# Two accumulator banks begun in spare PSUM banks, the old four copied out together, and one more unit by sums in the last round of the down projection

## The chip, the cores and the metric

One core of a Trainium2 chip runs the whole program. The metric is the device time in microseconds (us). TensorE (PE) does the matrix products; VectorE (DVE) and ScalarE (ACT) prepare its operands and move its results; GpSimd (POOL) issues the accumulating DMAs; SyncE (SP) issues the weight loads. The program gives each engine its instructions in a fixed order, so one that waits holds up those behind it on that engine.

## The reference

A block of one layer on 256 tokens of width 2048, all in float32:

- h = x + GLA(rmsnorm(x)), a chunked gated linear attention with its projections
- a = relu(rmsnorm(h) @ w_up), with w_up of 2048 x 8192
- h = h + (a * a) @ w_down, with w_down of 8192 x 2048
- the output is rmsnorm(h)

The change lies wholly in the product with w_down.

## The kernel before

**Operands in two parts.** Every weight tile is loaded as float32 into a tile `raw`. ACT casts it to `hi` (L118), DVE subtracts to get `lo` (L131 for plain loads, L165 for w_up, L998 for sums), and PE makes three products, hi*hi, lo*hi and hi*lo (L719). `raw` has seven buffers, used in turn; `hi` and `lo` have five.

**The order of the two projections.** The hidden width is cut into 8 rounds of 1024. `up()` makes the activations of a round in 16 steps; `down()` multiplies them with w_down. A round of `down` takes four groups g of 512 output columns, one pass per group, and each pass takes four units kp of 256 hidden rows. In the last round only g = 0 and g = 1 are done in this way; the other 1024 columns follow in eight steps of 128 rows, `last_step` (L1084), whose matmuls have line L176. `up` runs 18 steps ahead; while it has steps left, one up step is laid between the products of each unit, and at the end the units stand alone. In the code `alone` (L911) is true for these.

**A unit in two ways.** A plain unit makes eight block products, 24 matmuls of 256 columns. A unit *by sums* (`by_sums`, L694) makes seven, 21 matmuls, on four accumulators P16, B32, P57 and BX4 of one PSUM bank each (L858). It needs sums of weight blocks: a second DMA on POOL's queue adds one block onto another while loading (L934), DVE makes three more additions (L957 to L959), ACT casts the sums (two casts of 512 columns, L991), and DVE subtracts once more over 1024 columns (L998). The first nine matmuls use the plain blocks (`these`, L951), the other twelve the sums (`early` and `late`, L999 and L1000). For a unit that stands alone, these twelve are put off until after the next unit's first products (`pending`, L967 to L970). It also needs sums of activation blocks, made by `forms` (L818: three subtractions on DVE, L824) and split into two parts over 1024 columns instead of 512 by `form_parts` (L829: ACT L834, DVE L835). A unit gets those if any group of its round goes by sums in it.

**Changing groups.** When a pass begins with another group, the four accumulators of the former group must be copied out of their banks to SBUF (`settle`, L883) and those of the new group be copied in (`begin`, L867). Both go through `copy_end` (L844), a copy on ACT (L849). `copy_hi` and `copy_end` are chained, so that ACT takes casts and copies in just the order in which the program lists them. There are eight banks: four for the former group, four spare once `up` has given its own back.

**The last pass.** It is round 7, group 1. I call its units U0 to U3 (kp 0 to 3), the two units before it, of group 0, V2 and V3, and the eight steps behind it K0 to K7. Before the change V2, V3 and U2 go by sums; V3's twelve put-off matmuls run behind U0's, and U2's behind U3's. ACT's list is: cast U0; begin B32 and BX4; cast V3's sums; cast U1; cast U2; settle P16, begin P16; cast U3; settle P57, begin P57; cast U2's sums; copy in two banks of the last eight steps (`last_banks(0)`, L1022); settle B32 and BX4; cast K0; `last_banks(1)`; cast K1, and so on.

**At the end** stand the additions that undo the sums (`combine`, L1036), the squares and the product with the final gain, and five stores per token half.

Of the kernel before, what the change touches and what calls it, by code (L numbers as in the profile page):

```python
# [68 lines left out]
def tile_gla_mlp(ctx, tc, x, xt, cols, w_vg, w_in, w_gate, w_out, w_up, w_down, final_norm, out):  # L69
# [12 lines left out]
    def psum_bank(i, name="acc"):  # L82
        return psum.tile([P, 512], F32, tag=f"b{i}", name=name)
# [606 lines left out]
    def order_of(m):  # L690

        return range(GROUPS)[:: 1 if m % 2 else -1]

    def by_sums(m, g, kp):  # L694

        if m == ROUNDS - 1:
            return (g, kp) in ((0, 2), (0, 3), (1, 2))
        return m < ROUNDS - 2 or g != order_of(m)[-1] or kp == 1


# [113 lines left out]

    form = form.rearrange("p (f s) -> p f s", f=8)
    ways_of = lambda m, kp: {by_sums(m, g, kp) for g in range(GROUPS)}

    def forms(m, kp, s):  # L818
# [18 lines left out]
    def stationary(m, kp, f):  # L837
        return [acts[m][kp // 2][:, kp % 2, i, f] for i in range(2)]
# [5 lines left out]
    def copy_end(to, src):  # L844

        with tc.issue_after(last_hi[0].ins), ExitStack() as order:
            if last_end[0]:
                order.enter_context(tc.issue_after(last_end[0]))
            last_end[0] = nc.scalar.copy(to, src).ins  # L849
# [8 lines left out]
    P16, B32, P57, BX4 = range(4)  # L858

    def home(k, g):  # L860
        if k in (P16, P57):
            return sums[g][:, 1:3] if k == P16 else sums[g][:, 0::3]
        return h[:, k // 2, g * GT : (g + 1) * GT].rearrange("p (f s) -> p f s", f=2)
# [3 lines left out]
    def begin(k, g):  # L867
        i = free.popleft()
        bank = psum_bank(i)
        if k in (B32, BX4) or g in begun:  # L870
            copy_end(two(bank), home(k, g))
            used.add(bank.name)
        return i, bank
# [9 lines left out]
    def settle(*ks):  # L883

        for k in ks:
            late.pop(k, lambda: None)()

    def down(passes):
# [7 lines left out]
        for n, (m, g) in enumerate(passes):  # L896
            fresh = not n or passes[n - 1][1] != g
            if fresh:

                banks = ahead or ({} if n else {k: begin(k, g) for k in (B32, P16)})  # L900
                ahead = None
                if m == ROUNDS - 1:
                    flush()
            ends = n + 1 == len(passes) or passes[n + 1][1] != g
            first = min(kp for kp in range(KP) if by_sums(m, g, kp)) if fresh else None

            if fresh:
                quick = first == 0
            for kp in range(KP):
                last = ends and kp == KP - 1  # L910
                alone = units + LEAD >= UPS  # L911
                by_parts = by_sums(m, g, kp)

                def products(n, these, w, banks=banks, last=last):
# [23 lines left out]
                if fresh and quick and kp < 2:  # L938
                    pass
                elif fresh and kp == 0:  # L940
                    banks.update({k: begin(k, g) for k in (B32, BX4)})
                elif fresh and kp == first:
                    settle(P16)
                    banks[P16] = begin(P16, g)
                elif fresh and kp > first and P57 not in banks:
                    settle(P57)
                    banks[P57] = begin(P57, g)
                at = lambda f, m=m, kp=kp: stationary(m, kp, f)
                block = lambda i, n=1: slice(i * T, (i + n) * T)
                if by_parts:  # L950
# [70 lines left out]
                    else:  # L1021
                        last_banks(0)  # L1022
                if fresh and kp == first + alone and not quick:
                    settle(B32, BX4)
            if ends:

                def end(k, i, bank, g=g):
# [28 lines left out]
    for _ in down(passes):  # L1056
        next(steps, None)
# [34 lines left out]
    for kt in range(KL):  # L1092
        k = kt - KL + ROOM
# [87 lines left out]
```

## Time and profile before

| | |
|---|---|
| time, median of 3 runs | 1049.01 us (1048.44 to 1049.16) |
| the profiled execution | 1049.37 us |
| its span, first to last instruction | 1047.6 us |
| matmuls | 9094 |
| bytes moved by DMA | 225.21 MB, mean 215 GB/s |

The profiled execution is 0.36 us above the median. Its span leaves out 1.77 us around the first and the last instruction. A row of the timeline gives the start in us from the span's beginning, the time of the merged group in us, engine, line, operation, output <- input, shapes, count, and in brackets how long the engine was idle before it and whose event ended that. Since matmuls are pipelined, the group's time of PE runs past the start of the next; the distance between starts is what a group costs.

### The profile page before, as it was taken

What the parts mean: (1) busy time and instruction counts of PE and PEld (TensorE: products, weight loads), DVE (VectorE), ACT (ScalarE), POOL (GpSimd) and SP (SyncE); (2) the same over time, 40 slices, a digit from 0 to 9 for tenths busy, and PEclk for the clock granted to TensorE, in tenths of its full rate; (3) what the DMA queues carried; (4) which work ended last, traced back from release to release, by engine and by line L of the source; (5) the groups of instructions that cost most, each with busy time, mean ns of one, the idle gap of its engine ahead of it and who ended that gap; (6) DMA issues with size and microseconds to landing.
All of it is one profiled execution on the core that took longest, in us unless ns stands there. A gap on an engine that the chain in (4) does not pass through costs nothing. (4 is left out here: it accounts for less than half of the span.)

```text
span 1047.6 us, 23146 instructions
## 1 busy us (share of the span) xinstructions
PE 1038.4 (99%) x9094; PEld 1038.0 (99%) x9094; DVE 844.0 (81%) x1225; ACT 703.8 (67%) x1045; POOL 110.4 (11%) x151
## 2 busy tenths in 40 slices
PE   9999999999999999999999999999999999999997
PEld 9999999999999999999999999999999999999997
DVE  6668655656465566889999999999999999999887
ACT  6785544546455455668678678788778777777785
POOL 0000000010000001111121211121111111111100
PEclk9999999999999999999999999999999999999998
DMA  9957665555656676678888887888888988887772
GB/s 336 336 167 214 192 199 162 161 144 180 198 180 185 185 219 186 169 222 230 227 235 225 238 240 213 247 233 227 236 234 227 241 236 231 229 232 220 233 242 91
DMA packets 112718, 225.21 MB, mean 215 GB/s; under 512 B 10289, under 2 KB 25265, under 8 KB 112481
## 3 DMA queue, kind: packets, MB, share of 16 engines
q1 hardware_dynamic: 95808, 207.39, 64.0%
q0 software_dynamic: 16128, 14.69, 9.4%
q8 instruction: 71, 1.16, 0.4%
q10 hardware_dynamic: 672, 1.66, 0.4%
q14 instruction: 39, 0.31, 0.1%
HBM read 221.60 MB, written 2.10 MB: 214 GB/s over the span
## 5 line engine op out<-in xcount | busy, mean ns | idle before, releaser
L118 ACT CAST hi<-raw 128x768 fp32r<-128x768 f32 (+4 forms) x610 | 490.1, 846 | 278.4 <-PE acc L176 105.8
L131 DVE TENSOR_TENSOR lo<-raw,hi 128x768 fp32r<-128x768 f32 (+3 forms) x226 | 241.7, 1071 | 122.8 <-ACT hi L118 120.1
L719 PE MATMUL acc<-hi,act 128*128 128x256 f32 x1696 | 247.8, 276 | 0.0
L719 PE MATMUL up<-hh,hi 128*128 128x256 f32 x1024 | 239.1, 276 | 0.0
L719 PE MATMUL up<-hl,hi 128*128 128x256 f32 x1024 | 239.1, 276 | 0.0
L165 DVE TENSOR_TENSOR lo<-raw,hi 128x1024 fp32r<-128x1024 f32 x160 | 194.8, 1219 | 30.9 <-ACT hi L118 30.6
L719 PEld LDWEIGHTS acc<-hi,act 128*128 128x128 f32 x1696 | 217.7, 188 | 0.0
L719 PEld LDWEIGHTS up<-hl,hi 128*128 128x128 f32 x1024 | 192.3, 188 | 0.0
L719 PEld LDWEIGHTS up<-hh,hi 128*128 128x128 f32 x1024 | 192.3, 188 | 0.0
L934 POOL DMA_DIRECT2D raw<-in_w_down x112 | 98.6, 880 | 516.2 <-DMA raw<-in_w_down 224.9
L998 DVE TENSOR_TENSOR lo<-raw,hi 128x1024 fp32r<-128x1024 f32 x112 | 136.4, 1218 | 1.6 <-ACT hi L118 1.0
L719 PE MATMUL up<-hh,lo 128*128 128x256 f32 x1024 | 137.1, 276 | 0.0
L719 PE MATMUL acc<-lo,act 128*128 128x256 f32 x848 | 134.0, 276 | 0.0
L719 PEld LDWEIGHTS up<-hh,lo 128*128 128x128 f32 x1024 | 125.8, 188 | 0.0
L719 PEld LDWEIGHTS acc<-lo,act 128*128 128x128 f32 x848 | 113.4, 188 | 0.0
L176 PE MATMUL acc<-hi,xA 128*128 128x256 f32 (+1 forms) x728 | 102.3, 278 | 0.8 <-ACT hi L118 0.8
L176 PEld LDWEIGHTS acc<-hi,xA 128*128 128x128 f32 x728 | 92.1, 188 | 1.0 <-ACT hi L118 1.0
L176 PE MATMUL acc<-lo,xA 128*128 128x256 f32 (+1 forms) x364 | 57.5, 278 | 0.0
L957 DVE TENSOR_TENSOR raw<-raw 128x256 f32<-128x256 f32 x112 | 47.4, 423 | 2.9
L958 DVE TENSOR_TENSOR raw<-raw 128x256 f32<-128x256 f32 x112 | 47.4, 423 | 2.8
L216 PE MATMUL acc<-xA,hi 128*128 128x256 f32 x288 | 49.2, 276 | 0.0
L176 PEld LDWEIGHTS acc<-lo,xA 128*128 128x128 f32 x364 | 48.8, 188 | 0.0
(159 smaller groups left out, 1197.3 us busy)
## 6 DMA issues: line engine op xcount, KB each, us to landing
raw<-in_w_up SPq DMA_DIRECT2D x128, 512.0 KB, 4.4
raw<-in_w_down SPq DMA_DIRECT2D x224, 256.0 KB, 4.5
raw<-in_w_in SPq DMA_DIRECT2D x80, 512.0 KB, 3.9
raw<-in_w_out SPq DMA_DIRECT2D x32, 512.0 KB, 4.1
raw<-in_w_down POOLq DMA_DIRECT2D x112, 128.0 KB, 5.2
raw<-in_w_down SPq DMA_DIRECT2D x16, 512.0 KB, 4.7
raw<-in_w_vg SPq DMA_DIRECT2D x14, 520.0 KB, 8.6
h<-in_x SPq DMA_DIRECT2D x4, 512.0 KB, 7.5
```

Of the source, the lines that this page charges most:

```text
L118: last_hi[0] = nc.scalar.copy(to, raw)
L131: last_lo[0] = nc.vector.tensor_tensor(lo[:, s], raw[:, s], hi[:, s].bitcast(F32), op=ALU.subtract)
L165: last_lo[0] = nc.vector.tensor_tensor(to[1], dst, to[0].bitcast(F32), op=ALU.subtract)
L176: nc.tensor.matmul(o[:, m], x, w[:, m], start=first and c == 0, stop=last, skip_group_check=True)
L216: nc.tensor.matmul(o, u[:, i, s], m, start=kt == 0 and n == 0 and j % 2 == 0, stop=kt == KT - 1 and n == 2, skip_group_check=True,)
L719: newest[0] = nc.tensor.matmul(o, x, w, start=first, stop=last, skip_group_check=True).ins
L934: nc.gpsimd.dma_start(out=raw[:, :T], in_=src[:, 0, T:], accum_op=ALU.add)
L957: tt(u[:, 2], u[:, 0], u[:, 2], op=ALU.add)
L958: tt(u[:, 1], u[:, 2], u[:, 1], op=ALU.subtract)
L998: last_lo[0] = nc.vector.tensor_tensor(to[1][:, :G], u, to[0][:, :G].bitcast(F32), op=ALU.subtract)
```

## The change

Three edits. `by_sums` gains (1, 1) in the last round, so that U1 goes by sums too. In a pass whose first unit by sums stands alone, both P16 and P57 are begun at that unit, in spare banks, with nothing copied out ahead of them. And the copy-out at the end of the unit behind it now takes all four accumulators of the former group.

```diff
         if m == ROUNDS - 1:
-            return (g, kp) in ((0, 2), (0, 3), (1, 2))
+            return (g, kp) in ((0, 2), (0, 3), (1, 1), (1, 2))
...
                 elif fresh and kp == first:
-                    settle(P16)
-                    banks[P16] = begin(P16, g)
-                elif fresh and kp > first and P57 not in banks:
-                    settle(P57)
-                    banks[P57] = begin(P57, g)
+
+                    if alone:
+                        banks.update({k: begin(k, g) for k in (P16, P57)})
+                    else:
+                        settle(P16)
+                        banks[P16] = begin(P16, g)
...
                 if fresh and kp == first + alone and not quick:
-                    settle(B32, BX4)
+                    settle(P16, P57, B32, BX4)
```

Of the two passes that enter these branches (the first unit by sums is not kp 0), round 6, group 0 is not alone at that unit and has settled P16 and P57 by the last line, so its list stays as it was. Round 7, group 1 changes. Its list on ACT becomes: cast U0; begin B32 and BX4; cast V3's sums; cast U1 (768 columns); begin P16 and P57; cast U2; cast U1's sums; settle all four; cast U3; cast U2's sums; `last_banks(0)`; cast K0; and so on. U1's twelve put-off matmuls run behind U2's nine.

## The prediction

> **What bounds the kernel now.** I read the page first: its span and the busy shares.
>
> ```profile
> span 1047.6 us, 23146 instructions
> PE 1038.4 (99%) x9094; PEld 1038.0 (99%) x9094; DVE 844.0 (81%) x1225; ACT 703.8 (67%) x1045; POOL 110.4 (11%) x151
> ```
>
> A busy PE need not be PE at its peak, so next come the waits of PE, over the whole span:
>
> ```profile
> PE aux L249 <- DVE ones L246: 1.1, 1, 1.1
> PE acc L176 <- ACT hi L118: 0.8, 1, 0.8
> ```
>
> These two are all, 1.9 us, and both fall in the first 20 us. So time goes down only with matmuls that fall away, and goes up with whatever makes PE wait. Third, two stages that the edits touch (columns: stretch, its length, busy us and instructions of PE, PEld, DVE, ACT, POOL, then PE's clock, DMA share, GB/s):
>
> ```profile
> 970.00:980.00 10.00, 10.00 (x91) 10.00 (x90) 9.86 (x16) 6.55 (x11) 0.88 (x1) 1.00 0.71 215
> 1010.00:1015.00 5.00, 5.00 (x46) 5.00 (x46) 2.97 (x6) 4.40 (x8) 0.00 (x0) 1.00 0.70 256
> ```
>
> PE is full at clock 1.00 in both. DVE is nearly full where the activation sums of the last round are made (970 to 980), and ACT where the last pass changes its banks (1010 to 1015). Fourth, PE's order of time in the last pass:
>
> ```profile
> 1010.52 1.98 PE L719 MATMUL acc<-hi,act 128*128 128x256 f32 x16
> ...
> 1014.26 1.98 PE L719 MATMUL acc<-hi,act 128*128 128x256 f32 x16
> ...
> 1016.98 1.07 PE L719 MATMUL acc<-hi,act 128*128 128x256 f32 x8
> ...
> 1018.34 0.96 PE L176 MATMUL acc<-hi,act 128*128 128x256 f32 x7
> ```
>
> V3's put-off products end and U1 starts at 1010.52, U3 at 1014.26, U2's put-off products at 1016.98, K0 at 1018.34. U3's 24 matmuls take 1016.98 - 1014.26 = 2.72 us, 0.1133 us each.
>
> **The gain.** U1 plain is 24 matmuls, by sums 9 + 12 = 21: 3 x 0.1133 = 0.34 us less on PE, 0.03% of the time. No other matmul goes. Without waits PE's new dates are: U1's nine at 1010.52, U2's nine at 1011.54, U1's twelve at 1012.56, U3 at 1013.92, U2's twelve at 1016.64, K0 at 1018.00. Each input must be there by its date.
>
> **ACT's and DVE's queues in the last pass.** ACT's order of time before, then DVE's:
>
> ```profile
> 1005.76 2.83 ACT L118 CAST hi<-raw 128x512 fp32r<-128x512 f32 x4 [0.18 <-issue]
> 1010.60 0.59 ACT L849 COPY sums<-acc 128x512 f32<-128x512 f32 x1 [2.01 <-PE acc L719]
> 1011.09 0.60 ACT L849 COPY acc<-sums 128x512 f32<-128x512 f32 x1
> 1011.61 1.05 ACT L118 CAST hi<-raw 128x1024 fp32r<-128x1024 f32 x1
> 1012.56 0.59 ACT L849 COPY sums<-acc 128x512 f32<-128x512 f32 x1
> ...
> 1013.55 1.15 ACT L118 CAST hi<-raw 128x512 fp32r<-128x512 f32 x2
> 1014.59 1.12 ACT L849 COPY acc<-h 128x512 f32<-128x512 f32 x2
> 1015.64 1.08 ACT L849 COPY h<-acc 128x512 f32<-128x512 f32 x2
> 1016.59 1.07 ACT L118 CAST hi<-raw 128x1024 fp32r<-128x1024 f32 x1
> ```
>
> ```profile
> 1002.66 0.95 DVE L131 TENSOR_TENSOR lo<-raw,hi 128x768 fp32r<-128x768 f32 x1
> 1003.66 1.23 DVE L998 TENSOR_TENSOR lo<-raw,hi 128x1024 fp32r<-128x1024 f32 x1
> 1004.80 0.42 DVE L957 TENSOR_TENSOR raw<-raw 128x256 f32<-128x256 f32 x1
> ...
> 1008.20 2.09 DVE L131 TENSOR_TENSOR lo<-raw,hi 128x1024 fp32r<-128x1024 f32 x2
> 1010.32 0.43 DVE L957 TENSOR_TENSOR raw<-raw 128x256 f32<-128x256 f32 x1
> 1010.78 0.43 DVE L958 TENSOR_TENSOR raw<-raw 128x256 f32<-128x256 f32 x1
> 1011.13 0.42 DVE L959 TENSOR_TENSOR raw<-raw 128x256 f32<-128x256 f32 x1
> 1012.69 1.23 DVE L131 TENSOR_TENSOR lo<-raw,hi 128x1024 fp32r<-128x1024 f32 x1 [1.14 <-ACT hi L118]
> ```
>
> The row at 1010.60 is the wait that the edit moves: ACT stands 2.01 us before it may copy P16 of group 0 out, until PE ends V3's products, and U3's cast and U2's casts of sums stand behind. From one start to the next a copy in costs 0.52 us (1011.09 to 1011.61), a copy out 0.49 (1010.60 to 1011.09), two copies out 0.95, a cast of 1024 columns 0.95, two casts of 512 columns 1.04, two copies in 1.05. On DVE a lo of 768 columns costs 1.00 us, one of sums 1.14, the three additions 0.46, 0.35 and 0.34.
>
> Now the new order. *ACT:* V3's casts of sums from 1005.76 to 1006.80; U1's cast, now of 768 columns (about 0.78, what the 2.83 us leave for U2's), to 1007.6; P16 and P57 begun, 1.05, to 1008.65; U2's cast to 1009.4. *DVE:* U1's lo at 1008.20, its additions at 1009.20, 1009.66 and 1010.01. ACT may cast U1's sums once L958 is through (1010.1) and is done at 1011.2; PE wants them at 1012.56. DVE takes U2's lo at 1010.35, then U1's sums (L998) at 1011.35 to 1012.58; PE wants those after eight matmuls, at 1013.47.
>
> Then comes the step that costs. The four copies out stand between U1's casts of sums and U3's cast. PE has long given the banks back, so they start at 1011.2; they take 0.49 + 0.49 + 0.95 = 1.93 us; U3's cast runs from 1013.12 to 1014.17. PE is ready for U3 at 1013.92. With a hand-over of 0.03 us, as from ACT's cast (1011.61 + 1.05 = 1012.66) to DVE's row at 1012.69, **PE waits 0.28 us**. Behind, U2's sums are cast by 1015.2 (date 1016.64), `last_banks(0)` is copied in by 1016.2 and K0 cast by 1017.2 (date 1018.00; before, 1017.66 for 1018.34). DVE takes U3's lo at 1014.2 to 1015.4 (date 1016.0, after sixteen matmuls) and U2's sums to 1016.6 (date 1017.8). Nothing else is late.
>
> Bounds of this wait: 0, if ACT is 0.3 us faster than my pitches add up to; 0.8 us, if the copies take their full 0.59 each (0.4 more in all) and U1's additions come 0.1 later. I take 0.28, worked from the pitches of the same copies 1 to 5 us further on.
>
> The Trainium skill speaks against the copies out ("ScalarE: Activation LUTs", in the part on what the profile stage does: for ScalarE a destination in PSUM is faster than one in SBUF). The rows show 0.59 us out of and 0.60 us into PSUM, so no such difference here.
>
> **DMA.** U1's load becomes two issues on SP and an accumulating one on POOL, ahead of U2's. U2's issue on POOL and the landing of all these DMAs:
>
> ```profile
> 999.35 0.88 POOL L934 DMA_DIRECT2D raw<-in_w_down  x1 [4.45 <-DVE lo L131]
> ...
> DMA to landing us min/median/max: 3.1/5.2/7.7
> ```
>
> Even issued at 999.35, the slowest lands at 1007.1; U1's additions read it at 1009.20. Cost nothing, with 2 us of cover. U1's `raw` is now held until L998 ends at 1012.6, not 1009.4; K4 uses it next, and K5 takes U2's, free at 1016.6. The loads of K0 to K7 and the cast of K5:
>
> ```profile
> DMA to landing us min/median/max: 3.9/5.1/6.5
> ```
>
> ```profile
> 1024.69 1.04 ACT L118 CAST hi<-raw 128x1024 fp32r<-128x1024 f32 x1
> ```
>
> By the slowest, K4 is there at 1019.1 and K5 at 1023.1, 1.6 us before its cast. Cost nothing; past that cover ACT would wait for the excess.
>
> **The activation sums.** Round 7's kp 1 now needs three subtractions on DVE, and its split covers 1024 columns instead of 512:
>
> ```profile
> 916.49 0.42 DVE L824 TENSOR_TENSOR work<-work 128x256 f32<-128x256 f32 x1
> 916.82 0.95 DVE L131 TENSOR_TENSOR lo<-raw,hi 128x768 fp32r<-128x768 f32 x1
> 917.69 0.28 DVE L824 TENSOR_TENSOR work<-work 128x128 f32<-128x128 f32 x1
> ...
> 919.10 1.22 DVE L165 TENSOR_TENSOR lo<-raw,hi 128x1024 fp32r<-128x1024 f32 x1
> ...
> 969.50 0.96 DVE L131 TENSOR_TENSOR lo<-raw,hi 128x768 fp32r<-128x768 f32 x1 [0.39 <-ACT hi L118]
> ...
> 971.63 1.22 DVE L165 TENSOR_TENSOR lo<-raw,hi 128x1024 fp32r<-128x1024 f32 x1
> ...
> 974.24 0.68 DVE L835 TENSOR_TENSOR act<-work,act 128x512 fp32r<-128x512 f32 x1
> ...
> 979.03 1.22 DVE L998 TENSOR_TENSOR lo<-raw,hi 128x1024 fp32r<-128x1024 f32 x1
> ```
>
> ```profile
> 981.08 0.62 PE L719 MATMUL acc<-lo,act 128*128 128x256 f32 x4
> ```
>
> In an earlier round the subtractions are laid among the additions of a unit: 0.33 us for the first, and 2.28 us from L131 to L165 (916.82 to 919.10) where 969.50 to 971.63 is 2.13 without. The first falls into the idle 0.39 us before 969.50; 0.15 is left. The split goes from 0.68 to 1.23 us (the subtraction over 1024 columns at 1012.69), 0.55 more. So the sums' lo at 979.03 comes 0.70 us later. It ended at 980.25 for matmuls at 981.08, a cover of 0.83: no wait, by 0.13 us. From above: laid end to end the subtractions cost 0.42 + 0.28 + 0.28 = 0.98, less 0.39, plus 0.55, is 1.14, and PE waits 0.31 us. I take 0, by the interleaved rows. ACT's split costs about 0.45 us more, a cast of 1024 against one of 512, in a stage where it is busy 6.55 of 10 us.
>
> By the Trainium skill ("VectorE: DVE Perf Modes", section "The DRAIN you can't avoid") a DVE operation does not start before the pipe is empty; the sum by it would be that upper end, 0.31 us higher. The rows differ: L998 at 1003.66 lasts to 1004.89, and the next starts at 1004.80.
>
> **The sum.** -0.34 + 0.28 + 0 = -0.06 us: the profiled 1049.37 us (span 1047.6 and 1.77 around it) becomes 1049.31; the median of the runs, 0.36 lower, 1048.95.
>
> **Rivals.** *A, the forecast:* the four copies eat the gain: 1048.95; 45%. *B, the whole gain:* U3 is cast by 1013.92: 1049.01 - 0.34 = 1048.67. For it speaks that my margin is 0.25 us in a queue of 8 us; 25%. *C, DVE's cover at 980 is gone:* 0.31 us beside A, 1049.26, up to 1049.8 with the upper bounds of both; 18%. *D, the other side:* DVE gets U3's lo ahead of U1's sums. Then L998 ends at 1016.6 for a date of 1013.47, and PE waits 3.1 us: 1049.01 - 0.34 + 3.1 = 1051.8. It decides as soon as L998 stands behind that lo at all. For it: DVE's order is made anew, and no link puts U3's lo behind L998. Against: U3's cast follows U1's casts on ACT, so L998 can go 2.9 us earlier, and at 1003.66 V2's L998 went ahead of the next additions; 9%. *E, no effect:* ACT's and DVE's orders hide it all, or U1's path isn't taken: 1049.01; 3%.
>
> By the skill ("TensorE: Matmul & The Clock Gate", section "Part 1: The HAM clock gate") the clock halves after an idle window of about 3.4 us; D would come near that, and lose up to 1.7 us more, an estimate from that page. No row here shows so long a wait.
>
> **Range and chances.** A measurement of this kernel can tell about 0.2% (2.1 us) from no change. A, B, C and E lie within it; D, and a C that I have undersized, are slower. Faster by 2.1 us would need 19 matmuls less. Low 1048.3: B, less the 0.36 us by which a single run here differs from the median. High 1050.0: C's upper end and 0.2. Chances: same 0.88, slower 0.10, faster 0.02.
>
> **What would show it.** Right: three matmuls fewer, four copies out in a row behind U1's casts of sums, and a wait of PE for L118 of some 0.3 us at U3. Wrong: no wait there (B), one near 980 (C), or L998 behind U3's lo (D). A change beyond 1 us would mean a queue that I have missed.

## The result and the profile after

The kernel after takes 1050.49 us, the median of 22 runs (1049.14 to 1051.41). Beside it, on the same chip, the kernel before took 1049.01 us (22 runs, 1048.44 to 1049.53). The ratio is 1.0015 [1.0009, 1.0021]: slower by 1.5 us, inside the 0.2% that the prediction takes as no change, yet clear of zero. The forecast was 1048.95 us, with a range up to 1050.0 that does not hold it.

The page of the profiled execution has the three matmuls fewer, and a span that is shorter than before's 1047.6 us:

```profile
span 1047.0 us, 23159 instructions
PE 1038.6 (99%) x9091; PEld 1038.2 (99%) x9091; DVE 847.2 (81%) x1232; ACT 705.4 (67%) x1047; POOL 111.2 (11%) x152
```

That execution took 1049.14 us, and it is the one lowest of the 22; the others lie from 1050.22 to 1051.41 us. What this trace shows of the order of work holds for all of them; what the other 21 spend besides must be read from a second profile (experiment 1). The waits of PE over the whole span, then ACT's and PE's order of time in the last pass:

```profile
PE aux L249 <- DVE ones L246: 1.1, 1, 1.1
PE acc L719 <- ACT hi L118: 0.2, 1, 0.2
```

```profile
1009.66 1.14 ACT L118 CAST hi<-raw 128x512 fp32r<-128x512 f32 x2 [0.83 <-DVE raw L959]
1010.70 1.07 ACT L849 COPY sums<-acc 128x512 f32<-128x512 f32 x2
1011.66 1.09 ACT L849 COPY h<-acc 128x512 f32<-128x512 f32 x2
1012.61 2.12 ACT L118 CAST hi<-raw 128x1024 fp32r<-128x1024 f32 x3
```

```profile
1012.89 0.62 PE L719 MATMUL acc<-lo,act 128*128 128x256 f32 x4
1013.74 2.08 PE L719 MATMUL acc<-hi,act 128*128 128x256 f32 x16 [0.24 <-ACT hi L118]
1015.67 1.07 PE L719 MATMUL acc<-lo,act 128*128 128x256 f32 x8
1016.57 1.07 PE L719 MATMUL acc<-hi,act 128*128 128x256 f32 x8
```

ACT's list is as forecast: cast of U1's sums, four copies out in a row, cast of U3. (Lines from L957 on are one or more higher than in before: its L998 is L999 here.) The wait at U3 stands where the forecast put it, but it is larger. The bracket says 0.24 us idle; the cost is read from starts. U1's last four matmuls start at 1012.89, so U3's first was due 4 x 0.1133 = 0.45 later, at 1013.34, and came at 1013.74: 0.40 late. Its sixteen then take 1015.67 - 1013.74 = 1.93 us instead of 16 x 0.1133 = 1.81: the second matmul is late by another 0.11. In all 0.51 us. From 1015.67 on, eight matmuls take 1016.57 - 1015.67 = 0.90 us, 0.113 each, as before. So the gain and the wait leave this execution a loss of 0.17 us (0.51 - 0.34) behind U3, and 0.19 more come from a stretch near 981 us (experiments 1 to 3). That it is still 0.23 us below before's profiled execution goes with a wait that is missing, the 0.8 us at L176 that before's has in its first 20 us: from there up to 980 us PE runs 0.77 us ahead of before's.

One more cost lies outside the trace. The profiled time is 1049.14 us for a span of 1047.0, so 2.1 us lie around the span, where before has 1.77. This holds in every run: 2.05 to 2.18 us in the 22 of the kernel after, 1.72 to 1.82 in the 33 of before that stand beside experiment 1. That is 0.35 us more, which no view shows. Together, 0.17 + 0.19 + 0.35 = 0.71 us is about half of the 1.5 us of the median. (With the 0.77 off at the start, and 0.17 off at the end, where 7.43 us pass from the last matmul's start to the span's end for before's 7.60, it is the -0.23 of this execution.)

**The theories.** *The slow pace* (P): after a late operand PE does not merely start later; it goes on at some 0.118 us a matmul instead of 0.1133, for hundreds of matmuls. Its rivals: *the waits at their own length*, with a start of the program that varies between runs; and *the added work*, that is the activation sums on DVE and ACT or the additional DMAs. The expectations below put numbers to what each theory that stood at the time gives, in their own words and letters: 1 to 4 were written before P was thought of, and W in the later ones is "the waits at their own length".

### The profile page after: what moved, and what is told of

It is laid out like the page before. It is cut to its first block, busy times and chain, and to the rows that moved or that the text cites. A ratio compares the mean times of both kernels' runs of the same rounds, so it can differ in the third digit from the quotient of the medians.

```text
span 1047.0 us, 23159 instructions
## 1 busy us (share of the span) xinstructions
PE 1038.6 (99%) x9091; PEld 1038.2 (99%) x9091; DVE 847.2 (81%) x1232; ACT 705.4 (67%) x1047; POOL 111.2 (11%) x152
## 5 line engine op out<-in xcount | busy, mean ns | idle before, releaser
L999 DVE TENSOR_TENSOR lo<-raw,hi 128x1024 fp32r<-128x1024 f32 x113 | 137.7, 1218 | 0.9 <-ACT hi L118 0.3
L176 PE MATMUL acc<-hi,xA 128*128 128x256 f32 (+1 forms) x728 | 102.5, 279 | 0.0
L176 PEld LDWEIGHTS acc<-hi,xA 128*128 128x128 f32 x728 | 92.5, 189 | 0.0
L176 PE MATMUL acc<-lo,xA 128*128 128x256 f32 (+1 forms) x364 | 57.5, 278 | 0.0
L176 PEld LDWEIGHTS acc<-lo,xA 128*128 128x128 f32 x364 | 48.9, 188 | 0.0
```

Of the source, the lines that this page charges most:

```text
L176: nc.tensor.matmul(o[:, m], x, w[:, m], start=first and c == 0, stop=last, skip_group_check=True)
L999: last_lo[0] = nc.vector.tensor_tensor(to[1][:, :G], u, to[0][:, :G].bitcast(F32), op=ALU.subtract)
```

## The experiments

All ratios are to the kernel before on the same chip. "n" is the number of runs.

**1. The same kernel again** (the kernel after, word for word).

> The changed kernel once more, for a second trace. Its profiled execution took 1049.14 us, its median is 1050.49, so some 1.4 us lie where that one trace does not show them. Theory Q (queue of ACT): the four copies out hold U3's cast up longer in a usual execution: PE waits 1.5 to 2 us for L118 at U3. Theory C (cover of DVE): the activation sums use up the 0.13 us of cover near 980 us, and PE waits 1 to 2 us for DVE there. Theory O (neither): the time between U1's start and the first matmul of K0 stays 7.9 to 8.1 us, 970 to 990 shows no wait, and the time is lost at the start or the end of the run. Median 1050.0 to 1050.9 by all three; ratio to before 1.0010 to 1.0020.

Measured: 1050.61 us (1050.11 to 1051.62, n = 11), 1.0017 [1.0008, 1.0026]. The profiled run took 1050.58 us, span 1048.5. PE's order of time at U3, and the last group of its span:

```profile
1013.34 0.62 PE L719 MATMUL acc<-lo,act 128*128 128x256 f32 x4
1014.18 2.16 PE L719 MATMUL acc<-hi,act 128*128 128x256 f32 x16 [0.23 <-ACT hi L118]
1016.18 1.10 PE L719 MATMUL acc<-lo,act 128*128 128x256 f32 x8
1017.12 1.10 PE L719 MATMUL acc<-hi,act 128*128 128x256 f32 x8
...
1018.53 0.99 PE L176 MATMUL acc<-hi,act 128*128 128x256 f32 x7
...
1040.44 0.87 PE L176 MATMUL acc<-room,act 128*128 128x256 f32 x6
```

The wait is the same (1014.18 is 0.39 us after the due 1013.79), so Q's 1.5 to 2 us are not there; nor are C's 1 to 2 us near 980, and from U1's start (1010.39) to K0 it is 8.14 us, a little over what O gives. But here eight matmuls take 1017.12 - 1016.18 = 0.94 us instead of 0.90, and it stays so: from K0 to the last group, 186 matmuls on, 1040.44 - 1018.53 = 21.91 us, 0.1178 each, where the same two rows in the other profile of this program lie 21.08 us apart, 0.1133 each:

```profile
1017.93 0.96 PE L176 MATMUL acc<-hi,act 128*128 128x256 f32 x7
...
1039.01 0.84 PE L176 MATMUL acc<-room,act 128*128 128x256 f32 x6
```

The same matmuls, no wait between the rows, and 0.83 us more. The busy share cannot show it: PE is "busy" for all of both. The number of matmuls in a stretch of fixed length can. Columns: stretch, its length, PE busy us and matmuls, clock, DMA share, GB/s; before first, then this run:

```profile
981.00:985.00 4.00, 4.00 (x38) 1.00 0.78 274
...
1016.00:1036.00 20.00, 20.00 (x179) 1.00 0.23 70
```

```profile
981.00:985.00 4.00, 4.00 (x36) 1.00 0.80 270
...
1016.00:1036.00 20.00, 20.00 (x172) 1.00 0.25 80
```

172 for 179 at the same granted clock of 1.00: the clock was not lowered. From U3 to the end 228 matmuls run at this pace; 228 x 4.5 ns = 1.0 us. There is a second, short stretch, at 981. This is the slow pace. A luckier or worse start of the program cannot make it, since the lateness grows between rows of the same trace.

**2. Only the activation sums** (the kernel before, with U1's sums of activation blocks made and not used; U1 stays plain, all else as before).

```diff
-    ways_of = lambda m, kp: {by_sums(m, g, kp) for g in range(GROUPS)}
+    ways_of = lambda m, kp: {by_sums(m, g, kp) or (m, g, kp) == (ROUNDS - 1, 1, 1) for g in range(GROUPS)}
```

> The kernel before, with the activation sums of round 7's kp 1 made (three subtractions and a split over 1024 columns) and not used. Theory C: this alone costs the whole loss, 1050.2 to 1050.9 us, and PE waits near 980. Theories Q and O: 1048.9 to 1049.3, no wait of PE there.

Measured: 1049.35 us (1048.66 to 1051.78, n = 11), 1.0007 [0.9998, 1.0016]. The interval just holds 1, so the time alone proves nothing. The trace has the stretch at 981 (36 matmuls in the window), and none behind 986.5 (179 in the second window). So that stretch comes with the activation sums, and the share of the added work is small: the 56 matmuls from 980.34 on take 6.62 us, 0.27 more than at 0.1133 each, where before's, from 980.63 on, take 6.43, 0.08 more; that makes 0.19. Two of the eleven runs took 1051.7 and 1051.8 us; no trace shows what those two were.

**3. The change without the activation sums** (the kernel after; U1's twelve put-off matmuls take plain activation blocks as their stationary operand, so the sums of activations are left out of the computation for this unit).

```diff
-    ways_of = lambda m, kp: {by_sums(m, g, kp) for g in range(GROUPS)}
+    ways_of = lambda m, kp: {by_sums(m, g, kp) and (m, kp) != (ROUNDS - 1, 1) for g in range(GROUPS)}
...
-                at = lambda f, m=m, kp=kp: stationary(m, kp, f)
+                made = True in ways_of(m, kp)
+                at = lambda f, m=m, kp=kp, made=made: stationary(m, kp, f if made else A12 + f % 4)
```

> The changed kernel without the activation sums for U1: its sums' matmuls take plain activation blocks instead, so the result leaves the Winograd form out for this unit, and PE, ACT and DMA in the last pass do what they do in the changed kernel. Theory C: the loss is gone, 1048.8 to 1049.2 us. Theories Q and O: it stays, 1050.2 to 1050.9.

Measured: 1050.13 us (1049.44 to 1050.97, n = 11), 1.0011 [1.0002, 1.0020]. The stretch at 981 is gone (38 matmuls), the one from U3 to the end is there (172 in the window). The two are separate, and the one at U3 carries most of the loss.

What starts the one at 981 is a cover that is thinner than the order of matmuls says. DVE's `lo` of the sums, then PE, of the second profile of the kernel after:

```profile
979.43 1.22 DVE L999 TENSOR_TENSOR lo<-raw,hi 128x1024 fp32r<-128x1024 f32 x1
```

```profile
980.31 0.62 PE L719 MATMUL acc<-hi,act 128*128 128x256 f32 x4
980.77 0.67 PE L719 MATMUL acc<-lo,act 128*128 128x256 f32 x4
981.28 2.05 PE L719 MATMUL acc<-hi,act 128*128 128x256 f32 x16
983.16 1.10 PE L719 MATMUL acc<-lo,act 128*128 128x256 f32 x8
```

The lo ends at 980.65, and its matmuls start on their date, 980.77: a cover of 0.12 us, and the view of waits has no entry. Still the four take 0.51 us to the next start instead of 0.45, and the sixteen behind them 1.88 instead of 1.81. The wait for `lo` stands on the weight load (PEld), which runs about one matmul (0.11 us) ahead of its matmul. Its rows show it late:

```profile
980.20 0.53 PEld L719 LDWEIGHTS acc<-hi,act 128*128 128x128 f32 x4
980.70 0.54 PEld L719 LDWEIGHTS acc<-lo,act 128*128 128x128 f32 x4
```

Four loads from 980.20 on put that of `lo` at 980.20 + 4 x 0.1133 = 980.65; it starts at 980.70, 0.05 us after `lo` ended and as much late (0.04 without the rounding). In before the same two rows start at 980.52 and 980.97, which is on date. That so short a lateness starts the stretch fits experiment 6, which moves the lo earlier.

**4. The copy-out split in two** (the kernel after; P16 and P57 copied out where the four were, B32 and BX4 behind U2's sums and `last_banks(0)`).

```diff
-                    settle(P16, P57, B32, BX4)
+                    settle(P16, P57)
+                if fresh and kp == (KP - 1 if alone else first) and not quick:
+                    settle(B32, BX4)
```

> The changed kernel with only P16 and P57 copied out ahead of U3's cast, and B32 and BX4 behind last_banks(0), as before. U3's cast comes 0.95 us earlier, so PE's wait of 0.24 us and the slow start of U3 go: 0.3 to 0.5 us less than the changed kernel by the profiled execution. Theory Q: the whole loss and more is gone, 1048.5 to 1048.8 us. Theories C and O: 1050.0 to 1050.5.

Measured: 1050.40 us (1049.63 to 1051.01, n = 11), 1.0013 [1.0005, 1.0022]; the profiled run 1049.78. The wait at U3 is gone, as meant, but the copies moved make K0 late:

```profile
1017.18 1.23 DVE L131 TENSOR_TENSOR lo<-raw,hi 128x1024 fp32r<-128x1024 f32 x1 [1.60 <-ACT hi L118]
```

```profile
1017.52 0.96 PE L176 MATMUL acc<-hi,act 128*128 128x256 f32 x7
1018.46 0.51 PE L176 MATMUL acc<-lo,act 128*128 128x256 f32 x2
```

K0's lo ends at 1018.41; its matmul was due at 1017.52 + 7 x 0.1133 = 1018.31 and came at 1018.46, 0.15 late. From there 185 matmuls run at the slow pace (170 in the window), to 1040.2. So 0.15 us of wait has 185 x 4.5 ns = 0.83 us behind it, where 0.51 us had 1.0: not its length decides, but that it comes, and how many matmuls lie behind it. That speaks against waits at their own length. (This experiment did not take the waits away, so it could not yet say what the change is worth without them.)

**5. No wait at all in the last pass** (the kernel after; P16 and P57 copied out ahead of U3's cast, B32 and BX4 right behind it).

```diff
+                if fresh and alone and not quick and kp == KP - 1:
+                    settle(B32, BX4)
...
-                    settle(P16, P57, B32, BX4)
+                    settle(P16, P57)
+                    if not alone:
+                        settle(B32, BX4)
```

> The changed kernel, with P16 and P57 copied out ahead of U3's cast and B32 and BX4 right behind it. By the traces so far the loss is a slow cadence of PE (117.8 ns from one matmul to the next instead of 113.3) that begins when PE has waited and goes on long after. Theory P (the cadence persists after a wait): U3 and K0 come in time, so 0.5 us of waiting and 1.0 us of slow cadence go, while 0.2 us near 980 stay: 1048.7 to 1049.0 us. Theory W (only the waits themselves cost): 0.5 us less than the changed kernel, 1049.9 to 1050.1.

Measured: 1049.37 us (1048.91 to 1051.97, n = 11), 1.0010 [1.0001, 1.0018]. The profiled run took 1048.91, with a span of 1046.8 us; U3's cast is early and the pace holds:

```profile
1011.88 1.06 ACT L118 CAST hi<-raw 128x1024 fp32r<-128x1024 f32 x1
```

```profile
1013.56 1.98 PE L719 MATMUL acc<-hi,act 128*128 128x256 f32 x16
1015.38 1.07 PE L719 MATMUL acc<-lo,act 128*128 128x256 f32 x8
```

The cast ends 0.62 us ahead of PE, and the window has 178 matmuls. But the runs fall into two groups: six at 1048.91 to 1049.37 and five at 1050.88 to 1051.97, and the median lies in neither theory's range. The lower group fits the slow pace gone from the last pass, with the 0.35 us outside the span on top of P's figure. The upper one I did not expect. The stretch at 981 is still in this kernel.

**6. The stretch at 981 removed too** (experiment 5, with the split of U1's activation sums two up steps later).

```diff
-            return [start, lambda: make(0), lambda: split(0), lambda: make(1), lambda: split(1)]
+            rest = [lambda: None] * (2 * (m == ROUNDS - 1))
+            return [start, lambda: make(0), lambda: split(0), lambda: make(1), *rest, lambda: split(1)]
```

> As e5_no_wait, and the split of round 7's kp 1 is made two up steps later, where DVE has over 3 us of cover. Theory P: the slow stretch of 980 to 986 us goes too, 0.2 us: 1048.5 to 1048.8 us, the whole gain of 0.34. If the slow stretch there has another cause than the late lo of the sums, it stays and the time is that of e5_no_wait.

Measured: 1048.97 us (1048.52 to 1049.67, n = 11), 1.0000 [0.9991, 1.0009]. DVE's sums' lo (L1002 in this kernel) ends at 979.72 now, 1.26 us ahead of its matmuls, and they keep the pace:

```profile
978.50 1.22 DVE L1002 TENSOR_TENSOR lo<-raw,hi 128x1024 fp32r<-128x1024 f32 x1
```

```profile
980.98 0.62 PE L719 MATMUL acc<-lo,act 128*128 128x256 f32 x4
981.43 1.98 PE L719 MATMUL acc<-hi,act 128*128 128x256 f32 x16
```

981.43 - 980.98 = 0.45 us, 38 and 179 matmuls in the two windows. With both causes taken away the loss is gone, and no run is above 1049.67. The time misses P's 1048.5 to 1048.8, which has the forecast gain of 0.34 us in it. PE's rows do show that gain. The last group of this run, then of before:

```profile
1038.97 0.84 PE L176 MATMUL acc<-room,act 128*128 128x256 f32 x6
```

```profile
1039.42 0.84 PE L176 MATMUL acc<-room,act 128*128 128x256 f32 x6
```

From the matmuls of the sums' lo it is 1038.97 - 980.98 = 57.99 us here, and 1039.42 - 981.08 = 58.34 in before: 0.35 less. But around the span this kernel too has 2.07 to 2.16 us for before's 1.73 to 1.84, and that takes the gain back.

**7. The wait without the rest of the change** (the kernel before, U1 plain; P57, B32 and BX4 copied out ahead of U3's cast).

```diff
+                if fresh and kp == first and alone and not quick:
+                    settle(P57)
+                    banks[P57] = begin(P57, g)
+                    settle(B32, BX4)
```

> The kernel before, with U3's cast alone made late: P57 is copied out and in and B32 and BX4 are copied out ahead of it instead of behind it, so that it ends at about 1014.6 us for 1014.26. U1 stays plain, PE has the same 9094 matmuls. Theory W: 0.3 to 0.5 us slower than before, 1049.3 to 1049.5 us. Theory P: 1.2 to 1.6 us slower in most executions, 1050.1 to 1050.6 us, with 117.8 ns from U3 to the end.

Measured: 1050.32 us (1049.98 to 1051.25, n = 11), 1.0013 [1.0004, 1.0021].

```profile
1014.43 0.39 PE L719 MATMUL acc<-lo,act 128*128 128x256 f32 x2
1015.09 2.15 PE L719 MATMUL acc<-hi,act 128*128 128x256 f32 x16 [0.27 <-ACT hi L118]
1017.08 1.10 PE L719 MATMUL acc<-lo,act 128*128 128x256 f32 x8
```

U3 was due at 1014.66 and comes 0.43 late; behind it the slow pace to the end (172 in the window). Neither sums, nor DMAs, nor the new banks are in this kernel, and it loses 1.2 us by the medians (0.4 to 2.2 by the interval): a wait there suffices. The added work falls as the main cause.

**8. The unit by sums with the banks as before** (the kernel before, `by_sums` with (1, 1) and nothing else).

> The kernel before with (1, 1) added to the units by sums and nothing else: P16 is copied out and in at U1, P57 at U2. U1's first matmul waits for the copies, 1.1 us, U1's sums for P57, some 0.8 us, and U3's cast some 0.5 us. Theory W: 1049.0 - 0.34 + 0.2 + 2.4 = 1051.3 us. Theory P: 1.0 to 1.3 us more, 1052.2 to 1052.6.

Measured: 1052.60 us (1052.21 to 1053.29, n = 5), 1.0033 [1.0021, 1.0046]. PE's two longest waits in the last pass are 0.4 us for ACT's copies (L849) and 0.6 us for DVE's lo of sums (L998). ACT's copy-in of P16 now stands behind V3's end with the last three of U1's first nine matmuls waiting for it, and U1's sums come late; the slow pace holds in the whole window behind 1016 (172). So the spare banks do what the diff says: by the medians they save some 2 us (1.0033 against 1.0015) of what the extra unit by sums costs with the old order.

**9 and 10. A wait in mid-program, and the same with a step that ends the slow pace.** In every profile with a slow stretch at 981, the fast pace is back behind 986.5. Near 985 before itself has twelve matmuls of 120 ns, in an up step of the last round, and 113.3 ns behind them. The kernel loads the weights of such a step at shifted addresses (`even`, used in `up()` and handed to `pair_of`). In 9, ten spare copies of 512 columns on ACT ahead of unit 64's casts make one wait near 757 us. 10 adds one more shifted step, near 829 us.

```diff
+                if units == 64:
+                    junk = tmp.tile([P, 512], F32, tag="t512", name="junk", bufs=1)
+                    for _ in range(10):
+                        copy_end(two(junk), hth[:, :2, :].bitcast(F32))
```

```diff
-... else (6,) if (m, q) in ((ROUNDS // 2 - 1, 0), (ROUNDS - 1, 1)) else ()
+... else (6,) if (m, q) in ((ROUNDS // 2 - 1, 0), (5, 1), (ROUNDS - 1, 1)) else ()
```

> The kernel before with one late input in the middle: ten spare copies of 512 columns on ACT, some 5 us, ahead of the casts of unit 64, near 755 us. Nothing else changes, and all matmuls stay. PE waits 1 to 3 us there. Theory W: 1050 to 1052 us. Theory P: 117.8 ns from there to the next step whose weights lie at shifted addresses (the one of round 7 near 986 us): 230 us, some 2030 matmuls, 9.1 us more: 1059 to 1061 us.

> As e9_mid_wait, and one more up step in the order and at the shifted addresses that the kernel uses near 617 and 986 us, twelve steps behind the late input (near 818 us). Theory P with a reset by such a step: the slow stretch ends there, after 61 us: 2.4 us beside the wait, 1052.5 to 1055 us. If such a step resets nothing, the time is that of e9_mid_wait.

Measured: 9 took 1062.81 us (1062.54 to 1064.91, n = 4), 1.0135 [1.0119, 1.0150]; 10 took 1056.28 us (1056.06 to 1057.61, n = 4), 1.0071 [1.0054, 1.0088]. PE's windows of before, 9 and 10:

```profile
770.00:820.00 50.00, 50.00 (x443) 1.00 0.85 236
835.00:985.00 150.00, 150.00 (x1326) 1.00 0.82 230
```

```profile
762.00:766.00 4.00, 4.00 (x28) 0.73 0.49 127
770.00:820.00 50.00, 50.00 (x427) 1.00 0.83 232
835.00:985.00 150.00, 150.00 (x1276) 1.00 0.79 223
1001.00:1021.00 20.00, 20.00 (x179) 1.00 0.77 227
```

```profile
835.00:985.00 150.00, 150.00 (x1326) 1.00 0.82 230
```

One wait, and 9 runs at the slow pace (427 and 1276 matmuls for 443 and 1326) until the shifted step of the last round; behind it 179 in 20 us, the fast pace. In 10 the fast pace is back behind the added step: 427 matmuls again from 770 to 820, then 1326. The difference of 6.5 us between the two is the price of the pace from 829 to 1000 us: 171 / 0.1178 = 1450 matmuls x 4.5 ns = 6.5. Both times lie above P's ranges (by 1.8 and 1.3 us), in which the half clock shown below is missing: 9's loss of 13.7 us is some 2.8 of wait, at least 1.2 at the half clock, and 2004 matmuls from 764.2 to 1000 x 4.5 ns = 9.0. So the slow pace is a state that a late operand can start and a shifted step ended here. What in such a step does it, the address or the order of its two blocks, was not told apart; nor, in 9 and 10, whether the wait or the half clock behind it started the pace. In 1, 4 and 7 the clock stayed at 1.00.

A late operand is not the only start. Before itself has the pace where no wait of PE is on record. At 177.98 it goes over from twelve matmuls of 128 columns (L518) to those of 256, in a projection of the attention. The slow pace lasts, with another such twelve in between, until twelve matmuls at 120 ns, from 190.91 to 192.35; behind them it is 113.3 again. Before's windows:

```profile
179.00:183.00 4.00, 4.00 (x36) 1.00 0.51 158
193.00:197.00 4.00, 4.00 (x38) 1.00 0.49 142
```

9's row at 762 shows something besides: 28 matmuls at a clock of 0.73, where before has 38 at 1.00. The wait is this:

```profile
756.23 0.62 PE L719 MATMUL acc<-lo,act 128*128 128x256 f32 x4
759.47 0.97 PE L719 MATMUL acc<-hi,act 128*128 128x256 f32 x6 [2.62 <-ACT hi L118]
```

PE stood 2.6 us. Its clock in finer windows of 9:

```profile
760.50:760.70 0.20, 0.20 (x2) 1.00 0.28 41
...
760.80:764.00 3.20, 3.20 (x17) 0.50 0.09 7
764.20:766.00 1.80, 1.80 (x18) 1.00 0.88 255
```

The clock is still 1.00 up to 760.7, 1.2 us after the wait, then halved from 760.8 to 764.0 at least, and 1.00 again from 764.2. By the Trainium skill ("TensorE: Matmul & The Clock Gate", section "Part 1: The HAM clock gate") the clock halves after an idle window of about 3.4 us, and comes back after a busy one as long. The length of the stretch agrees: at least 3.2 us, and at most the 3.5 from 760.7 to 764.2. The first figure does not: 2.6 us of idling sufficed, and PE had been at work again for 1.2 us when the clock fell. The waits of 0.15 to 0.6 us in the last pass of the other runs left it at 1.00.

**11 and 12. Experiments 5 and 6 again**, 11 to see the upper group of 5 in a trace.

> e5_no_wait once more, for a second trace: its runs fell in two groups, 1048.9 to 1049.4 and 1050.9 to 1052.0 us. Theory P: a run of the upper group has 117.8 ns from 980 us past the shifted step at 986 to the end, some 480 matmuls, 2.1 us; one of the lower group has 113.3 from 986 on, as e5_no_wait.

> e6_late_split once more, for its place against the kernel before: its PE does three matmuls less and has no stretch of slow cadence that the kernel before lacks, which is 0.34 us. Theory P: median 1048.5 to 1049.0 us, no run above 1050; the first runs gave 1048.97 beside 1049.13. 0.03% is less than the interval can hold apart.

Measured: 11 took 1048.75 us: the lower group once more, with the stretch at 981 (36 matmuls) and none behind (179). 12 took 1049.13 us (1048.64 to 1049.73, n = 11), 1.0001 [0.9992, 1.0010], a little above P's 1048.5 to 1049.0. So the version of 6 equals before, and no version here beats before measurably; the interval is wider than the 0.34 us. The upper group of 5 was not seen in a trace. Its 1.9 us would fit the slow pace not ended by the shifted step but kept to the end (about 480 matmuls x 4.5 ns = 2.1 us), and 5 of the 12 runs of this kernel belong to it, while 6, which has no slow stretch for that step to end, has none in 22. That stays an argument; the cause of the group is open.

**The time around the span.** It is 2.05 to 2.19 us in all runs of the kernel after and of 4, 5, 6, 8, 11 and 12, and 1.72 to 1.84 us in all of before and of 2, 3, 7, 9 and 10. The first are the kernels whose U1 multiplies with sums of activation blocks; they are also the longest programs (23158 to 23160 instructions against 23146 to 23156). Which of the two it goes with was not tested, and the cause is open.

## Why the prediction was wrong

- **The gain: right.** Three matmuls fell away, 0.34 us by the rows.
- **The orders of ACT and DVE: right.** Four copies stand in a row, and no wait of PE for L999, the former L998, shows.
- **The wait at U3: right in place, too small in size.** 0.51 us for 0.28. U3's cast ended at 1013.69, 0.35 us behind PE's date where the pitches gave 0.25, the hand-over to PE took 0.05 us (1013.69 to 1013.74) where I took 0.03 from ACT to DVE, and the second matmul lost 0.11. The bounds, 0 to 0.8, held it.
- **The activation sums: right in the cover, wrong in what it means.** I gave "no wait, by 0.13 us"; the cover came out at 0.12. But I counted it to the matmul. The weight load wants `lo` about 0.11 us earlier. Cost 0.19 us (0.27 against 0.08), with the slow pace up to 986.
- **DMA: right.** No wait of PE for a load in any profile of the kernel after.
- **The step that failed is the sum.** It rests on the sentence that time "goes up with whatever makes PE wait", and prices a wait at its own length. The wait at U3 cost 0.51 us and then 228 x 4.5 ns = 1.0 us behind it, a term that the sum does not have. A second one it put at nothing without a reason: it took the 1.77 us around the span over unchanged, and they became 2.12, 0.35 more. With measured terms: -0.34 + 0.51 + 0.19 + 1.0 + 0.35 = +1.71, so 1049.01 becomes 1050.72; the two medians are 1050.49 and 1050.61. Of the difference some 0.15 us is the shorter end of the program (7.43 and 7.45 us in the two traces of the kernel after, 7.60 in before's). In the forecast's terms, -0.34 + 0.28 + 0 = -0.06.
- **The rivals.** A's queue of copies is what happened, but its price lacked the pace behind the wait and the time around the span: it is 1.5 us too low. C's place showed beside it, in a form that its price (0.31 us of wait) did not have. B, D and E did not come by the rows. The slow pace was in none of them, and so not in the range; it could have been looked for, since before has it: 36 matmuls for 38 in 4 us at 179 (above), twelve matmuls from 16.91 to 18.35 at 0.120 us each, and the up step at 986 with 0.120, all at clock 1.00. So the sentence that only matmuls and waits move PE's time did not hold in before's own trace.

## What to carry to other kernels

On a PE that is full, compare the distance between starts of equal matmuls, or their number in windows of equal length, not the busy share: 99% busy was read in two runs of one program that differed by 1.4 us (1049.14 and 1050.58). Price a wait of PE not by its length alone but by how many matmuls follow until the pace comes back, if it brings the slow one; near the end of a program that may be more than the wait, and in the middle far more. And keep the cover to the weight load: one matmul's length and a hand-over more than the matmuls' dates say. Compare time minus span as well: a kernel can gain in its span and lose as much around it (6).

## What the runs showed of the hardware

- PE had three paces for the same 128 x 256-column matmul at granted clock 1.00: 113.3, 117.8 and, in the shifted steps and some of the projection's, 120 ns. The Trainium skill ("TensorE: Matmul & The Clock Gate", section "Back-to-back issue gap") gives one spacing at full clock for 256 columns, so it has no place for this.
- A wait of 0.15 us (4), or a weight load late by some 0.04 us (1), was enough to bring the slow pace; it lasted over some 2000 matmuls in 9. In before it also came with a change of the matmuls' shape (178 us), with no wait on record.
- A wait does not always bring it: the first profiled run of the kernel after had the wait at U3 and the fast pace behind it. One of 33 timed runs of that program lies below 1050.1 us. Why this one kept the pace is open.
- The time around the span, 1.72 to 1.84 us in every run of before, was 2.05 to 2.19 in every run of the kernels with 12 to 14 instructions more than its 23146; the cause is open.
